# Projection products between the transposes of attention, and products of 512 columns in halves

## The chip, the cores and the metric

The kernel runs on one core of one Trainium2 chip. Its engines are named as in the profile: PE is TensorE (matmuls), PEld its weight loads, DVE is VectorE, ACT is ScalarE, POOL is GpSimd, and SP only issues transfers. The metric is the device time of one execution in microseconds, as the median of the runs; lower is better. Before the change it was 425.61 us, the median of three runs from 425.08 to 425.87.

## The reference: what is computed

One decoder block on x of 512 rows by 1024 columns, all in float32:

```python
h = rms_norm(x, norm_g)
proj = h @ w_in          # fq fk fv fz mq mk mv mz (512 each), ga gb (1024 each), fl (8)
y_fox  = fox_attention(rms(fq), rms(fk), fv, log_sigmoid(fl + b_f)) * silu(fz)
y_moba = moba_attention(rope(rms(mq)), rope(rms(mk)), mv) * silu(mz)
merged = sigmoid(ga + b_gate[0]) * (y_fox @ w_fox) + sigmoid(gb + b_gate[1]) * (y_moba @ w_moba)
out = x + merged @ w_out
```

Each branch has 8 heads of width 64. Both attentions are causal over 512 positions. With 512 positions and three blocks chosen out of two, the block choice of the second branch leaves plain causal attention.

## The kernel before, in words

**Number format.** TensorE multiplies in a reduced float32 format. So each operand is split into a high part and a low part, and every product of two matrices is three matmuls into the same accumulator: high by high, high by low, low by high. In the text "product" is one such matmul. A product of 256 columns has a moving side of 128 x 256, one of 512 columns a moving side of 128 x 512; the stationary side is always 128 x 128 and is loaded by a weight load of its own (PEld).

**Units.** The projections are cut into units. A unit of q, k or v (`unit`) takes 128 rows of the input and 256 weight columns: 8 chunks of the contraction by 3 products are 24 products of 256 columns, into one accumulator bank of the pair `pj`, and then a copy out by ACT and DVE. A unit of the z columns (`unit_z`) takes 128 weight columns and all 512 rows: 24 products of 512 columns. A unit of the w_fox product (`unit_f`) is 12 products of 512 columns. Before a unit, `pump` issues the loads and splits of the weight chunks that are due up to three chunks ahead of it.

**Attention.** It goes in four groups: heads 0 to 3 of the first branch ("fa"), heads 4 to 7 ("fb"), then the same of the second branch ("ma", "mb"). A group consists of pieces. `Tr` turns q and k of two heads by 8 transposes of 128 x 128 into two banks (`p_qT`, `p_kT`, L530 and L532), from which ACT and DVE make QS, KH and KL (L539 to L547). `Aa` computes the logits of a head in four row blocks (`lg`, L572 and L573), the softmax numerators with DVE (L575) and Exp on ACT (L577). `Bb` turns the numerators by 10 transposes of 128 x 128 (`p_a` four, `p_b` four, `p_cc` two, L617), splits them (`pth` by ACT at L623, `ptl` by DVE at L624) and multiplies them with v (`pv`, L627 and L628). `Yp` normalises and multiplies with the z gate. A transpose is a matmul whose stationary side is the data and whose moving side is an identity of 128 columns.

**What sets the order.** The program mixes the pieces of a group with the units listed for it: `inter` alternates between the two lists in proportion to their lengths, a whole unit or a whole piece at a time. Group fa is filled with units of fqb, fkb, fvb and mqa; fb with mka, mva and mza; ma with mqb, mkb and mvb; mb with mzb (two units of 512 columns) and wf0 to wf2 (six). The units of wf3 follow alone. The program's order is then the order of preference only: when the kernel is built, a scheduler puts the instructions of each engine in the order in which it expects their inputs, so that in the built program products of a unit already stand between logits and pv matmuls. `behind(engine)`, that is `tc.issue_after`, ties an instruction to stand after the last one given to that engine so far. Every engine, TensorE too, works off its instructions in the built order, and waits at an instruction whose inputs are not ready.

**After attention** come the gate products (`pb_GA`, `pb_GB`, L767 to L770), the w_moba product (`pm`) and the output product (`po`).

Of the kernel before, what the change touches and what calls it, by code (L numbers as in the profile page):

```python
# [13 lines left out]
P = 128  # L14
# [15 lines left out]
def fox_moba_kernel(ctx: ExitStack, tc, xT, x, w_in, w_fl, w_fox, w_moba, w_out, cst, rope, out):  # L30
# [60 lines left out]
    def col(c, n=1):  # L91
        return cs[:, c:c + n]
# [212 lines left out]
        for i, (a, b) in enumerate(pairs):  # L305
            T.matmul(o, a, b, start=(i == 0), stop=(i == n - 1))

    def unit_mm(p, name, t, hfs=(0, 1), first=True, last=True):
        n = 264 if name == "fka" else CW
        for hf in hfs:  # L310
            hi, lo = chunks[name][hf]
            for k in range(4):
                kk = 4 * hf + k
                st = slice(t * P, (t + 1) * P)
                T.matmul(p[:, :n], Gh[:, kk, st], hi[:, k, :n], start=(kk == 0), stop=False)
                T.matmul(p[:, :n], Gh[:, kk, st], lo[:, k, :n], start=False, stop=False)
                T.matmul(p[:, :n], Gl[:, kk, st], hi[:, k, :n], start=False, stop=(kk == KT - 1))

    def evac_qk(p, name, t):
        if name not in QN:  # L320
# [75 lines left out]
    def unit(name, t):  # L396
        def go():
            p = pj(f"pj_{name}{t}")
            unit_mm(p, name, t)
            if name[1] == "v":  # L400
                evac_v(p, name, t)
            else:
                evac_qk(p, name, t)
        return go


    def tr_mm(p, name, c):
        cc = slice(c * P, (c + 1) * P)
        for hf in range(2):
            hi, lo = chunks[name][hf]  # L410
            for k in range(4):
                kk = 4 * hf + k
                gh, gl = Z[kk] if name[0] == "f" else (Gh[:, kk, :], Gl[:, kk, :])
                T.matmul(p, hi[:, k, cc], gh, start=(kk == 0), stop=False)
                T.matmul(p, hi[:, k, cc], gl, start=False, stop=False)
                T.matmul(p, lo[:, k, cc], gh, start=False, stop=(kk == KT - 1))

    ZS = {}

# [2 lines left out]
    def unit_z(name, c):  # L422
        def go():
            p = (tp if name == "fzb" else pj)(f"pz_{name}{c}")
            tr_mm(p, name, c)
            z = t2("y", 15, f"zs_{name}{c}")
            s = t2("y", 15, "sg") if name == "mzb" else t2("u", 4, "sg")
            if name[0] == "f":
                V.tensor_tensor(out=z, in0=p, in1=rbc, op=OP.mult)
                A.activation(s, z, AF.Tanh, scale=0.5)  # L430
                V.scalar_tensor_tensor(z, s, 1.0, z, op0=OP.add, op1=OP.mult)
            else:
                A.activation(s, p, AF.Tanh, scale=0.5)
                V.scalar_tensor_tensor(z, s, 1.0, p, op0=OP.add, op1=OP.mult)
            ZS[name[0], 2 * (name[2] == "b") + c] = z
        return go


    LR = con.tile([64, S], F32R, name="LR")
# [77 lines left out]
    def attn_group(br, half, gq, gk):  # L517
# [8 lines left out]
        def Tr(pr):  # L526
            def go():
                pq, pk = tp("p_qT"), tp("p_kT")
                for t in range(NT):
                    T.transpose(pq[:, t * P:(t + 1) * P], qn[:, t, pr * P:(pr + 1) * P], ident)  # L530
                for t in range(NT):
                    T.transpose(pk[:, t * P:(t + 1) * P], kn[:, t, pr * P:(pr + 1) * P], ident)  # L532
                for o in range(2):
                    h = 2 * pr + o
                    me, ot = (slice(0, HD), slice(HD, P)) if o == 0 else (slice(HD, P), slice(0, HD))
                    qs = t2("qs", 4, "QS", dt=F32R)
                    kh = t2("qs", 4, "KH", dt=F32R)
                    kl = KLt[o][pr]
                    A.activation(qs[me, :], pq[me, :], AF.Copy, scale=gq[me, :])  # L539
                    V.scalar_tensor_tensor(qs[ot, :], pq[me, :], gq[me, :], qs[me, :].bitcast(F32),  # L540
                                           op0=OP.mult, op1=OP.subtract)
                    A.activation(kh[me, :], pk[me, :], AF.Copy, scale=gk[me, :])
                    if direct:
                        A.activation(kh[ot, :], pk[me, :], AF.Copy, scale=gk[me, :])  # L544
                    else:
                        nc.scalar.dma_start(out=kh[ot, :].bitcast(F32), in_=kh[me, :].bitcast(F32))
                    V.scalar_tensor_tensor(kl[me, :], pk[me, :], gk[me, :], kh[me, :].bitcast(F32),  # L547
                                           op0=OP.mult, op1=OP.subtract)
                    q2 = qs
                    if fox:  # L550
                        q2 = Q2t[o]
                        lr = slice(HD, HD + 4) if o == 0 else slice(0, 4)
                        hh = hb + h
                        nc.sync.dma_start(out=q2[lr, :].bitcast(F32), in_=LR[hh:32:8, :].bitcast(F32))
                        nc.sync.dma_start(out=kl[lr, :].bitcast(F32), in_=LR[32 + hh:64:8, :].bitcast(F32))
                        if direct:
                            V.tensor_copy(q2[me, :], qs[me, :].bitcast(F32))
                        else:
                            nc.scalar.dma_start(out=q2[me, :].bitcast(F32), in_=qs[me, :].bitcast(F32))
                    st[h] = (qs, kh, kl, q2)  # L560
            return go
# [48 lines left out]
        def Bb(h):  # L610
            def go():
# [2 lines left out]
                pv = pst("pv", 1, "pv")  # L614

                def blk(dst, i, j):
                    T.transpose(dst, pts[i][:, j * P:(j + 1) * P], ident)  # L617

                def spl(p, n):
                    tag, w, bufs = ("pt", 512, 4) if n == 512 else ("pc", 256, 2)  # L620
# [67 lines left out]

    FS, MG = {}, {}

    def br_mm(p, name, br, c):
        hi, lo = chunks[name][0]
        cc = slice(c * P, (c + 1) * P)
        for k in range(4):
            yh, yl = Y[br, k]
            T.matmul(p, hi[:, k, cc], yh, start=(k == 0), stop=False)  # L696
            T.matmul(p, hi[:, k, cc], yl, start=False, stop=False)  # L697
            T.matmul(p, lo[:, k, cc], yh, start=False, stop=(k == 3))  # L698

    def unit_f(i, c):  # L700
        def go():
            j = 2 * i + c
            p = pj(f"pf{j}")
            br_mm(p, f"wf{i}", "f", c)
            if j == 0:
                f = sb.tile([P, 4, S], F32, name="f03", tag="v", bufs=2)
                FS[0], FS[1] = f[:, 0:2, :], f[:, 2:4, :]
            elif j in (4, 6):
                FS[j // 2] = sb.tile([P, 2, S], F32, name=f"f{j}", tag="qk", bufs=4)
            A.activation(FS[i][:, c, :], p, AF.Copy)  # L710
        return go
# [121 lines left out]
    def merge_a(i, c):  # L833
        if True:
            j = 2 * i + c
            p = pj(f"pm{j}")
            br_mm(p, f"wm{i}", "m", c)
            u = SG[i][:, c, :]
            V.tensor_tensor(out=u, in0=p, in1=u, op=OP.mult)
            V.tensor_tensor(out=u, in0=u, in1=FS[i][:, c, :], op=OP.add)  # L840
# [180 lines left out]
            return [unit_z(name, c) for c in range(2)]  # L1021
        return [unit(name, t) for t in range(4)]

    def filler(names):
        res = []
        for nm in names:
            for n, u in enumerate(units(nm)):
                def go(i=first_prep[nm] + (n if nm[0] == "G" else 0), u=u):
                    pump(i)
                    u()  # L1030
                res.append(go)
        return res

    def inter(a, b):
# [30 lines left out]
    for k, u in enumerate(fz):  # L1065
        u()
        if k < 3:
# [7 lines left out]
            ("f", "b", C_FQ, C_FK, ["mka", "mva", "mza"]),  # L1075
            ("m", "a", C_MQ, C_MK, ["mqb", "mkb", "mvb"]),
            ("m", "b", C_MQ, C_MK, ["mzb", "wf0", "wf1", "wf2"]))
    head, body, tail, gate = attn_group("f", "a", col(C_FQ), col(C_FK))
    head[0]()
    for n in range(4):  # L1080
        nxt = []

        def following(n=n, nxt=nxt):
            br, half, cq, ck = plan[n + 1][:4]
            if n == 1:
                moba_begin()
            nxt.extend(attn_group(br, half, col(cq), col(ck)))
            nxt[0][0]()
        fill = filler(plan[n][4])
        if n == 0:  # L1090
            for k in range(4):
                store = []

                at = 3 * k

                def with_sums(u=fill[at], k=k, store=store):
                    u()
                    with tc.issue_after(last_on(mybir.EngineType.DVE)):
                        store.append(make_sums(k))

                def with_store(u=fill[at + 1], store=store):
                    u()
                    store[0]()
                fill[at], fill[at + 1] = with_sums, with_store
        inter(body + ([following] if n < 3 else []) + tail, fill)
        if n < 3:
            at = 2
            body, tail = nxt[1][:at] + gate + nxt[1][at:], nxt[2]
            gate = nxt[3]
    seq(["wf3"])  # L1110
    enter("gates")
    load_sums()
    fill = filler(["GA0", "GA1", "GB0"])
# [123 lines left out]
```

## Time and profile before

| What | Value |
|---|---|
| median of three runs | 425.61 us |
| the profiled execution, in all | 425.94 us |
| its span, first to last instruction | 424.2 us |
| granted TensorE clock | 0.999 |
| busy PE, PEld, DVE, ACT, POOL | 417.8, 388.6, 327.4, 279.2, 103.8 us |
| matmuls recorded | 2913 |
| attention stage, about | 66 to 285 us |

The page lists busy time by engine, then the span in 40 slices, the transfers, the chain of work that ended last, and groups of instructions. A group's row gives the line, engine and operation, what is written from what, the shapes and the count, then busy time and the mean of one in ns, then the engine's idle time before them and what ended it. A row of the timeline begins with the start in us from the span's start and the duration in us; several equal instructions in a row are one row with a count. Matmuls overlap in the records and their ends are modelled, so what a matmul takes is read from the distance between starts. A row of busy time by stretch gives the stretch and its length, then busy time and count for each engine, the granted clock, the share of the transfer engines and GB/s.

### The profile page before, as it was taken

What the parts mean: (1) busy time and instruction counts of PE and PEld (TensorE: products, weight loads), DVE (VectorE), ACT (ScalarE), POOL (GpSimd) and SP (SyncE); (2) the same over time, 40 slices, a digit from 0 to 9 for tenths busy, and PEclk for the clock granted to TensorE, in tenths of its full rate; (3) what the DMA queues carried; (4) which work ended last, traced back from release to release, by engine and by line L of the source; (5) the groups of instructions that cost most, each with busy time, mean ns of one, the idle gap of its engine ahead of it and who ended that gap; (6) DMA issues with size and microseconds to landing.
All of it is one profiled execution on the core that took longest, in us unless ns stands there. A gap on an engine that the chain in (4) does not pass through costs nothing.

```text
span 424.2 us, 7682 instructions
## 1 busy us (share of the span) xinstructions
PE 417.8 (98%) x2913; PEld 388.6 (92%) x2913; DVE 327.4 (77%) x574; ACT 279.2 (66%) x527; POOL 103.8 (24%) x120
## 2 busy tenths in 40 slices
PE   8999999999999999999999999999999999999996
PEld 6998899999999998899998888899999989988885
DVE  3779977799967778678666679767979698689883
ACT  4976326778777878569757687656756535686450
POOL 1065630225235550015660100340000000022230
PEclk9999999999999999999999999999999999999999
DMA  7972334667253033212032310673052703697484
GB/s 233 392 281 87 112 100 111 181 206 199 74 176 114 26 102 100 80 45 99 27 100 68 106 53 27 229 250 117 24 178 62 236 2 110 208 259 118 99 140 159
DMA packets 24340, 56.10 MB, mean 132 GB/s; under 512 B 2808, under 2 KB 7600, under 8 KB 24304
## 3 DMA queue, kind: packets, MB, share of 16 engines
q1 hardware_dynamic: 13392, 38.11, 27.9%
q0 software_dynamic: 3392, 8.39, 8.7%
q10 hardware_dynamic: 7520, 9.11, 6.7%
q8 instruction: 23, 0.38, 0.4%
q14 instruction: 13, 0.11, 0.1%
HBM read 48.11 MB, written 6.32 MB: 128 GB/s over the span
## 4 chain that ended last, share of the span: by engine, by line
PE 96%; DMA 1%; SPq 0%; DVE 0%; issue 0%; ACT 0%
PE pb_GB L770 3%; PE pb_GA L770 3%; PE pb_GA L767 3%; PE pb_GB L767 3%; PE pb_GB L769 3%; PE pb_GA L769 3%; PE po L958 3%; PE po L957 3%; PE po L956 3%; PE pv L628 2%; PE lg L573 2%; PE pv L627 2%; PE lg L572 2%; PE pf L697 2%; PE pf L696 2%; PE pm L698 2%
## 5 line engine op out<-in xcount | busy, mean ns | idle before, releaser
L343 POOL TENSOR_TENSOR ff<-ss,mh 128x8 f32<-128x8 f32 x16 | 31.6, 1981 | 71.4 <-DVE ss L341 62.9
L575 DVE CUSTOM_DVE_ANT_0 p<-lg,mask 128x128 f32<-128x128 f32 (+1 forms) x64 | 30.9, 487 | 16.1 <-PE lg L573 15.6
L577 ACT ACTIVATE p<-p,negm 128x128 f32<-128x128 f32 (+1 forms) x64 | 35.7, 559 | 10.9 <-DVE negm L575 10.0
L905 POOL DMA_DIRECT2D wr_o<-in_w_out_dram x4 | 4.9, 1294 | 95.5 <-ACT wr_o L904 95.5
L143 DVE TENSOR_TENSOR wl_GA<-wr_ga,wh_GA 128x1024 fp32r<-128x1024 f32 x14 | 16.9, 1223 | 5.8 <-ACT wh_GA L141 3.9
L141 ACT ACTIVATE wh_GA<-wr_ga 128x1024 fp32r<-128x1024 f32 x14 | 14.7, 1061 | 9.9 <-PE pb_GA L769 5.1
L141 ACT ACTIVATE wh_GB<-wr_gb 128x1024 fp32r<-128x1024 f32 x14 | 14.6, 1059 | 9.5 <-PE pm L697 3.5
L918 ACT ACTIVATE wh_o<-wr_o 128x1024 fp32r<-128x1024 f32 x14 | 14.8, 1060 | 7.9 <-PE pb_GB L769 2.8
L572 PE MATMUL lg<-KH,QS 128*128 128x128 f32 (+1 forms) x64 | 20.0, 324 | 0.0
L919 DVE TENSOR_TENSOR wl_o<-wr_o,wh_o 128x1024 fp32r<-128x1024 f32 x14 | 17.0, 1222 | 3.8 <-ACT wh_o L918 3.8
L143 DVE TENSOR_TENSOR wl_GB<-wr_gb,wh_GB 128x1024 fp32r<-128x1024 f32 x14 | 16.9, 1222 | 3.5 <-ACT wh_GB L141 3.5
L653 DVE TENSOR_TENSOR ypair<-pv,ysh 64x512 f32<-64x512 f32 x16 | 11.0, 687 | 6.7 <-ACT ysh L652 6.3
L547 DVE SCALAR_TENSOR_TENSOR KL<-p_kT,cs,KH 64x512 fp32r<-64x512 f32 x16 | 12.0, 749 | 3.4 <-ACT KH L544 3.2
L652 ACT ACTIVATE ysh<-pv 64x512 f32<-64x512 f32 x16 | 9.5, 594 | 7.3 <-PE pv L628 4.2
L624 DVE TENSOR_TENSOR ptl<-p_a,pth 128x512 fp32r<-128x512 f32 x16 | 11.0, 685 | 4.2 <-ACT pth L623 4.2
L337 DVE TENSOR_REDUCE ss<-sq 128x8 f32<-128x512 f32 x16 | 10.9, 681 | 4.0 <-ACT sq L336 3.9
L767 PE MATMUL pb_GA<-Gh,wh_GA 128*128 128x256 f32 x48 | 13.6, 284 | 0.0
L769 PE MATMUL pb_GA<-Gl,wh_GA 128*128 128x256 f32 x48 | 13.5, 281 | 0.0
L770 PE MATMUL pb_GA<-Gh,wl_GA 128*128 128x256 f32 x48 | 13.5, 281 | 0.0
L770 PE MATMUL pb_GB<-Gh,wl_GB 128*128 128x256 f32 x48 | 13.5, 281 | 0.0
L769 PE MATMUL pb_GB<-Gl,wh_GB 128*128 128x256 f32 x48 | 13.4, 281 | 0.0
L767 PE MATMUL pb_GB<-Gh,wh_GB 128*128 128x256 f32 x48 | 13.3, 281 | 0.0
(461 smaller groups left out, 1801.8 us busy)
## 6 DMA issues: line engine op xcount, KB each, us to landing
wr_ga<-in_w_in_dram SPq DMA_DIRECT2D x8, 512.0 KB, 3.8
wr_gb<-in_w_in_dram SPq DMA_DIRECT2D x8, 512.0 KB, 4.6
wr_o<-in_w_out_dram SPq DMA_DIRECT2D x8, 512.0 KB, 11.4
xt<-in_xT_dram SPq DMA_DIRECT2D x8, 256.0 KB, 7.3
x<-in_x_dram SPq DMA_DIRECT2D x8, 256.0 KB, 6.0
s_dramh<-sum_sh ACTq DMA_DIRECT2D x8, 256.0 KB, 5.6
s_draml<-sum_sl ACTq DMA_DIRECT2D x8, 256.0 KB, 2.5
wr_wf<-in_w_fox_dram SPq DMA_DIRECT2D x4, 512.0 KB, 3.2
```

Of the source, the lines that this page charges most:

```text
L141: A.activation(hi[:, :, 0:n], src, AF.Copy)
L143: eng.tensor_tensor(out=lo[:, q, 0:n], in0=src[:, q], in1=hi[:, q, 0:n].bitcast(F32), op=OP.subtract)
L343: G.tensor_tensor(out=f2, in0=ss.rearrange("p t h -> p (t h)"), in1=mh, op=OP.pow)
L572: T.matmul(lg[:, :n], qs[:, qt], kh[:, :n], start=True, stop=False)
L575: V.tensor_tensor_reduce(pt, lg[:, :n], mask[:, 512 - n:512], -0.125, 3.0e38, op0=OP.add, op1=OP.min, accum_out=mkn[:, hh, i:i + 1])
L577: A.activation(pt, pt, AF.Exp, bias=mkn[:, hh, i:i + 1], scale=-1.0, accum_out=rs[:, hh, i:i + 1])
L767: T.matmul(o, hi[:, k, cc], lh, start=(n < 3 and c == 0 and k == 0), stop=False, skip_group_check=True)
L769: T.matmul(o, hi[:, k, cc], ll, start=False, stop=False, skip_group_check=True)
L770: T.matmul(o, lo[:, k, cc], lh, start=False, stop=(k == 3), skip_group_check=True)
L918: A.activation(wide(hi), wide(R[key, c]), AF.Copy)
L919: V.tensor_tensor(out=wide(lo), in0=wide(R[key, c]), in1=wide(hi).bitcast(F32), op=OP.subtract)
L956: T.matmul(o, gh, hi[:, c, r, :], start=(new and k == 0), stop=False, skip_group_check=True)
```

## The change

1. The functions that issue products of units become generators: they hand over one product at a time. `products` issues them as before; `halves` issues each product of 512 columns as two of 256 columns, on the two halves of the same bank and with the same stationary side. `halves` is used for mzb and for all of wf0 to wf3; mza and the z units before attention stay whole, as do the products of w_moba.
2. The units of all four groups are made before attention and also put into one list, `AHEAD`, in their order. `turn` replaces the calls of transpose in `Tr` and `Bb`. After each transpose it gives out up to three products of the first unfinished unit in that list; with the last of them come the unit's copies. All transposes but the first of a `Tr` or a `Bb` are tied to stand behind the last TensorE instruction so far, which as a rule is the third such product. The products themselves are not tied: the scheduler may put them elsewhere. A unit begun in this way is finished when its turn comes in `inter`; one that is already done then issues nothing, except that `pump` is called for it at that place.

```diff
-    def unit_mm(p, name, t, hfs=(0, 1), first=True, last=True):
+    def unit_mm(name, t):
         n = 264 if name == "fka" else CW
...
+        st = slice(t * P, (t + 1) * P)
+        for kk in range(KT):
+            hi, lo = (w[:, kk % 4, :n] for w in chunks[name][kk // 4])
+            gh, gl = Gh[:, kk, st], Gl[:, kk, st]
+            yield from ((gh, hi), (gh, lo), (gl, hi))
+
+    def halves(p, pairs):
+
+        pairs = list(pairs)
+        n = 2 * len(pairs)
+        for i in range(n):
+            a, b = pairs[i // 2]
+            c = slice(i % 2 * CW, (i % 2 + 1) * CW)
+            if i:
+                yield
+            T.matmul(p[:, c], a, b[:, c], start=(i == 0), stop=(i >= n - 2), skip_group_check=True)
+
+    def products(o, pairs):
+
+        pairs = list(pairs)
+        for i, (a, b) in enumerate(pairs):
+            if i:
+                yield
+            T.matmul(o, a, b, start=(i == 0), stop=(i == len(pairs) - 1))
...
     def unit(name, t):
         def go():
             p = pj(f"pj_{name}{t}")
-            unit_mm(p, name, t)
+            yield from products(p[:, :264 if name == "fka" else CW], unit_mm(name, t))
...
     def unit_z(name, c):
         def go():
             p = (tp if name == "fzb" else pj)(f"pz_{name}{c}")
-            tr_mm(p, name, c)
+            yield from (halves if name == "mzb" else products)(p, tr_mm(name, c))
...
+    AHEAD = []
+
+    def turn(o, i, first):
+        if first:
+            T.transpose(o, i, ident)
+        else:
+            with behind(mybir.EngineType.PE):
+                T.transpose(o, i, ident)
+        for n in range(3):
+            while AHEAD and AHEAD[0].done:
+                AHEAD.pop(0)
+            if AHEAD:
+                AHEAD[0].step()
+
+    class Unit:
+        def __init__(self, i, go):
+            self.i, self.go, self.it, self.done = i, go, None, False
+
+        def step(self):
+            if self.it is None:
+                self.it = self.go()
+            if self.it is None or next(self.it, self) is self:
+                self.done = True
+
+        def run(self):
+            pump(self.i)
+            while not self.done:
+                self.step()
...
                 for t in range(NT):
-                    T.transpose(pq[:, t * P:(t + 1) * P], qn[:, t, pr * P:(pr + 1) * P], ident)
+                    turn(pq[:, t * P:(t + 1) * P], qn[:, t, pr * P:(pr + 1) * P], t == 0)
                 for t in range(NT):
-                    T.transpose(pk[:, t * P:(t + 1) * P], kn[:, t, pr * P:(pr + 1) * P], ident)
+                    turn(pk[:, t * P:(t + 1) * P], kn[:, t, pr * P:(pr + 1) * P], False)
...
                 def blk(dst, i, j):
-                    T.transpose(dst, pts[i][:, j * P:(j + 1) * P], ident)
+                    turn(dst, pts[i][:, j * P:(j + 1) * P], j == 0 and i == 0)
...
     def unit_f(i, c):
         def go():
             j = 2 * i + c
             p = pj(f"pf{j}")
-            br_mm(p, f"wf{i}", "f", c)
+            yield from halves(p, br_mm(f"wf{i}", "f", c))
...
-    def filler(names):
+    def filler(names, ahead=False):
         res = []
         for nm in names:
             for n, u in enumerate(units(nm)):
-                def go(i=first_prep[nm] + (n if nm[0] == "G" else 0), u=u):
-                    pump(i)
-                    u()
-                res.append(go)
+                x = Unit(first_prep[nm] + (n if nm[0] == "G" else 0), u)
+                if ahead:
+                    AHEAD.append(x)
+                res.append(x.run)
         return res
...
+    fills = [filler(p[4], True) for p in plan]
+    wf3 = filler(["wf3"])
...
-        fill = filler(plan[n][4])
+        fill = fills[n]
...
-    seq(["wf3"])
+    for u in wf3:
+        u()
```

More of the change, by code (lines that the diff above doesn't have):

```diff
@@ L306, in mm3 @@
             T.matmul(o, a, b, start=(i == 0), stop=(i == n - 1))
-    def unit_mm(p, name, t, hfs=(0, 1), first=True, last=True):
+    def unit_mm(name, t):
         n = 264 if name == "fka" else CW
[L310 to L317, printed above, removed]
+        st = slice(t * P, (t + 1) * P)
[18 more added lines that the diff above has]
+            T.matmul(o, a, b, start=(i == 0), stop=(i == len(pairs) - 1))
     def evac_qk(p, name, t):
@@ L404, in unit, with tr_mm @@
         return go
-    def tr_mm(p, name, c):
+    def tr_mm(name, c):
         cc = slice(c * P, (c + 1) * P)
[L409 to L416, printed above, removed]
+        for kk in range(KT):
+            hi, lo = (w[:, kk % 4, cc] for w in chunks[name][kk // 4])
+            gh, gl = Z[kk] if name[0] == "f" else (Gh[:, kk, :], Gl[:, kk, :])
+            yield from ((hi, gh), (hi, gl), (lo, gh))
     ZS = {}
@@ L689, in fox_moba_kernel, with br_mm @@
     FS, MG = {}, {}
-    def br_mm(p, name, br, c):
+    def br_mm(name, br, c):
         hi, lo = chunks[name][0]
@@ L695, in br_mm @@
             yh, yl = Y[br, k]
-            T.matmul(p, hi[:, k, cc], yh, start=(k == 0), stop=False)
-            T.matmul(p, hi[:, k, cc], yl, start=False, stop=False)
-            T.matmul(p, lo[:, k, cc], yh, start=False, stop=(k == 3))
+            yield from ((hi[:, k, cc], yh), (hi[:, k, cc], yl), (lo[:, k, cc], yh))
     def unit_f(i, c):
@@ L836, in merge_a @@
             p = pj(f"pm{j}")
-            br_mm(p, f"wm{i}", "m", c)
+            for _ in products(p, br_mm(f"wm{i}", "m", c)):
+                pass
             u = SG[i][:, c, :]
```

## The prediction

> **What bounds the kernel now.** I read the profile in this order: the page's busy table and chain, then who waited for whom on TensorE, then the busy time by stretch, then single rows of the timeline, to price each kind of step.
>
> ```profile
> span 424.2 us, 7682 instructions
> PE 417.8 (98%) x2913; PEld 388.6 (92%) x2913; DVE 327.4 (77%) x574; ACT 279.2 (66%) x527; POOL 103.8 (24%) x120
> PEclk9999999999999999999999999999999999999999
> PE 96%; DMA 1%; SPq 0%; DVE 0%; issue 0%; ACT 0%
> ```
>
> TensorE is busy for 98% of the span and carries 96% of the chain that ended last, at a full granted clock. The list of what TensorE waited for has three rows only, all at lines of the head of the kernel:
>
> ```profile
> PE warm_ps L107 <- DVE fg_pre L480: 1.5, 1, 1.5
> PE fqa L392 <- DVE wl_fqa L168: 0.7, 1, 0.7
> PE fqa L391 <- ACT Zh L131: 0.6, 1, 0.6
> ```
>
> The attention stage, where the change lies, has this busy time in its four head groups (columns: us, then PE, PEld, DVE, ACT, POOL busy):
>
> ```profile
> 66.00:118.00 52.00, 52.00 (x427) 51.22 (x426) 46.91 (x101) 40.66 (x88) 13.00 (x9) 1.00 0.56 161
> 118.00:172.00 54.00, 54.00 (x408) 51.53 (x408) 40.59 (x87) 42.14 (x90) 22.19 (x30) 1.00 0.30 98
> 172.00:225.00 53.00, 53.00 (x419) 51.37 (x418) 35.41 (x77) 37.69 (x83) 21.48 (x26) 1.00 0.22 70
> 225.00:285.00 60.00, 60.00 (x349) 52.25 (x349) 45.31 (x85) 44.04 (x91) 10.31 (x12) 1.00 0.37 123
> ```
>
> TensorE never waits there: 219 of 219 us. So there is no stall for a new order to close, and the time changes only by what a step costs on TensorE, or by a stall that the new order opens. DVE in the first group (46.91 of 52) is the nearest cover to give way.
>
> **What one step costs.** Ends of matmuls are modelled, so I use differences of starts. Products, first and last of runs of one width:
>
> ```profile
> 53.78 0.28 PE L315 MATMUL pj_fva<-wh_fva,Gh 128*128 128x256 f32 x1
> 59.92 0.28 PE L316 MATMUL pj_fva<-wl_fva,Gh 128*128 128x256 f32 x1
> ...
> 236.68 0.40 PE L414 MATMUL pz_mzb<-Gh,wh_mzb 128*128 128x512 f32 x1
> 240.18 0.40 PE L414 MATMUL pz_mzb<-Gh,wh_mzb 128*128 128x512 f32 x1
> ...
> 290.74 0.28 PE L769 MATMUL pb_GA<-Gl,wh_GA 128*128 128x256 f32 x1
> 333.22 0.28 PE L770 MATMUL pb_GB<-Gh,wl_GB 128*128 128x256 f32 x1
> ```
>
> 52 steps of 256 columns in 6.14 us are 0.1181 us each; 358 in the gates stage in 42.48 us are 0.1187; 15 steps of 512 in the last head group in 3.50 us are 0.2333. Transposes, ten and four in a row between products of 256, then one alone between products of 512 (with a stationary side of 8 columns), and last the step of 384 columns:
>
> ```profile
> 96.72 0.28 PE L317 MATMUL pj_fkb<-wh_fkb,Gl 128*128 128x256 f32 x1
> 96.84 0.60 PE L617 MATMUL p_a<-ident,p 128*128 128x128 f32 x4
> 97.27 0.60 PE L617 MATMUL p_b<-ident,p 128*128 128x128 f32 x4
> 97.71 0.38 PE L617 MATMUL p_cc<-ident,p 128*128 128x128 f32 x2
> 97.85 0.37 PE L315 MATMUL pj_fvb<-wh_fvb,Gh 128*128 128x256 f32 x1
> 98.05 0.28 PE L316 MATMUL pj_fvb<-wl_fvb,Gh 128*128 128x256 f32 x1
> ...
> 123.62 0.29 PE L317 MATMUL pj_mqa<-wh_mqa,Gl 128*128 128x256 f32 x1
> 123.74 0.60 PE L617 MATMUL p_a<-ident,p 128*128 128x128 f32 x4
> 124.30 0.28 PE L315 MATMUL pj_mqa<-wh_mqa,Gh 128*128 128x256 f32 x1
> ...
> 174.77 0.39 PE L628 MATMUL pv<-ptl,v_fvb 128*128 128x512 f32 x1
> 175.00 0.27 PE L597 MATMUL p_ri<-ident,rinv 128*8 128x128 f32 x1
> 175.34 0.39 PE L414 MATMUL pz_mza<-Gh,wh_mza 128*128 128x512 f32 x1
> ...
> 235.08 0.34 PE L572 MATMUL lg<-KH,QS 128*128 128x384 f32 x1
> 235.25 0.34 PE L573 MATMUL lg<-KL,QS 128*128 128x384 f32 x1
> ```
>
> From 96.72 to 98.05 are 1.33 us; less two products of 256 (0.236) that is 1.094 for ten, 0.109 each. From 123.62 to 124.30 it is 0.68 less 0.236, 0.444 for four, 0.111 each. From 174.77 to 175.34 it is 0.57 less two products of 512 (0.467): 0.10 for one alone. So a transpose costs about 0.11 us wherever it stands, though its 128 columns would stream in 0.06: steps of 256, 384 and 512 take 0.118, 0.17 and 0.233, some 0.058 more for each 128. The reason is in the rows of weight loads:
>
> ```profile
> 123.64 0.46 PEld L617 LDWEIGHTS p_a<-ident,p 128*128 128x128 f32 x4
> ...
> 174.54 0.19 PEld L628 LDWEIGHTS pv<-ptl,v_fvb 128*128 128x128 f32 x1
> 174.77 0.08 PEld L597 LDWEIGHTS p_ri<-ident,rinv 128*8 128x8 f32 x1
> 175.00 0.19 PEld L416 LDWEIGHTS pz_mza<-Gh,wl_mza 128*128 128x128 f32 x1
> ```
>
> The load for 174.77 is over after 0.08 us, and the next load starts only at 175.00, when the transpose itself starts. Loads run one ahead and no further, so the load behind a transpose cannot hide under the long product before it.
>
> **The change part by part.** (a) *Halves.* In the built order the matmuls of 512 columns fall from 602 to 458 and those of 256 rise from 1840 to 2128: 144 products (48 of mzb, 96 of wf0 to wf3) become 288. Both halves have the same stationary side; the page counts 2913 loads for 2913 matmuls although the products at L414 and L415 follow each other on the same wh, so I count a load for every half. A pair costs 2 x 0.1187 against 0.2333, +0.0041 us; times 144 that is +0.59 us. I take the gates row, since there too the stationary side is a weight and the moving side the input. By the projection row it is 2 x 0.1181 - 0.2333 = 0.0029, +0.42; the end below is 0 (the columns are the same), the one above 0.0064 x 144 = +0.92, should the 512s it replaces run at the 0.2314 that they show elsewhere:
>
> ```profile
> 31.56 0.39 PE L414 MATMUL pz_fza<-Zh,wh_fza 128*128 128x512 f32 x1
> 53.55 0.39 PE L416 MATMUL pz_fzb<-Zh,wl_fzb 128*128 128x512 f32 x1
> ```
>
> (95 steps in 21.99 us.)
>
> (b) *Products behind transposes.* Both orders hold 243 transposes; before they stand in 62 unbroken runs (most of 4, five of 10), after in 150, of which 115 are of one. Total work is the same; only the edges of runs multiply, by 88. The edge has a price: the load of the four at 123.64 starts 0.02 after the product at 123.62, where the loads at 174.77 and 175.00 start with the matmul before them; the first transpose stands at 123.74, 0.12 after the product. Ten in a row at 1.094 and four at 0.444 give 0.108 per transpose and 0.011 per run, with rounding as large as the edge. I take 0.006 per run, about half: 88 x 0.006 = +0.53 us; ends 0 and 0.011 x 88 = +0.97. A transpose behind a product of 384 or 512 shows no edge (0.10 above), but only about 20 of the 150 runs stand so.
>
> (c) *Moved work.* The first projection products start earlier, and the transposes of a head spread over up to nine gaps of three products (9 x 0.354 = 3.2 us). What reads them, the copies at L623 and L624 and QS and KH at L539 to L547, starts that much later, and the pv and lg matmuls behind those. TensorE works in one order, so a transpose that waits for its Exp (L577) now holds the products tied in behind it, and a pv that waits holds the next unit. I cost this at nothing: projection products still stand between, and the waits list shows TensorE never reaching a transpose, pv or lg too soon. The price without that cover is the second rival. ACT, DVE, POOL and SP keep their operations; SP and POOL get no new transfer, and a weight chunk is read at most a few products earlier than before.
>
> Sum: 0.59 + 0.53 = +1.12 us. The profiled execution took 425.94 us in all (span 424.2), so 427.06 for one like it; the median of the three runs is 425.61, 0.33 below, so 426.7. A difference of 0.2%, 0.85 us, is about what a measurement of this kernel tells from no change.
>
> The Trainium skill, page "TensorE: Matmul & The Clock Gate", section "Back-to-back issue gap", says that loads and matmuls are pipelined through a 64-deep reorder window and that a stream at 128 columns runs at about 81 ns a matmul. By that figure 150 transposes whose following load is hidden would cost 0.029 us less each, an estimate of -4.3 us, against +0.53 by the rows. The trace does not agree: 0.109 each in the run of ten, and the load at 175.00 waited.
>
> **The rivals.** *Hidden loads (faster).* If two loads could be ahead, three products and a transpose would cost four loads, 4 x 0.109 = 0.436, and not 3 x 0.118 + 0.111 = 0.465: -0.029 for 127 such places, -3.7, with the halves -3.1: 422.5 us. It decides as soon as the load behind a transpose starts before that transpose. Against it stands the row at 175.00; for it, only that the one such row quoted has an 8-column load.
>
> *A stall in the first group (slower).* DVE is busy for 90% of it, and each head passes three copies at L624:
>
> ```profile
> L624 DVE TENSOR_TENSOR ptl<-p_a,pth 128x512 fp32r<-128x512 f32 x16 | 11.0, 685 | 4.2 <-ACT pth L623 4.2
> ```
>
> If the spread transposes make half such a copy late (0.34 us) for each of four heads, TensorE waits 1.4 us at pv: 428.1. In the other groups DVE and ACT have more than 11 us to spare.
>
> *Hardly anything happens (within 0.2%).* The products are only offered; the build decides, and 93 of 181 pairs of neighbouring transposes remain. If an edge costs nothing and the halves 0.42, the time is 426.0.
>
> **How the numbers follow.** No stall, steps as priced: 0.60, 426.7 with its own range 426.1 to 427.5. A stall besides: 0.15, 428.1. Edges free: 0.14, 426.0. Hidden loads: 0.11, 422.5. The range 425.3 to 428.6 leaves out the last case and little else. About a sixth of the first case lies under +0.85 us; with the third that gives 0.24 for no visible change, 0.65 for slower, 0.11 for faster.
>
> **What would show it.** Right: the list of TensorE's waits still ends with the head of the kernel, a single transpose between products of 256 costs 0.11 to 0.12, two halves 0.236 to 0.238, the end of the gates run (333.22 before) comes about 1.1 us later, and the rest of the span is as long as before. Wrong: a weight load that starts before the transpose ahead of it (faster), a row for pv, lg or pf in TensorE's waits (slower still), or halves that share a load, 144 loads fewer than matmuls.

## The result, and the profile after

The changed kernel took 428.26 us (median of 4 runs, 428.07 to 428.45), the kernel before 425.58 us (median of 4 runs on the same chip, 425.08 to 425.87). The ratio is 1.0064, with a 95% interval of 1.0047 to 1.0082: 2.68 us slower, where 1.12 was forecast.

First the page of the changed kernel: its busy times and the chain that ended last (the span is 426.5 us).

```profile
PE 419.7 (98%) x3057; PEld 396.0 (93%) x3057; DVE 328.4 (77%) x574; ACT 278.7 (65%) x527; POOL 106.4 (25%) x120
PE 91%; DVE 3%; DMA 3%; ACT 1%; issue 1%; SPq 0%; ACTq 0%; DVEq 0%
```

TensorE still is the bound. There are 3057 loads for 3057 matmuls, so no half shares a load. But the chain, which was 96% TensorE with 1% in transfers, now runs for 3% through DVE and for 3% through transfers. The list of what TensorE waited for (us in total, times, longest) names the places:

```profile
PE warm_ps L107 <- DVE fg_pre L523: 1.5, 1, 1.5
PE fqa L408 <- DVE wl_fqa L168: 0.6, 1, 0.6
PE lg L615 <- DMA KH<-KH: 0.5, 1, 0.5
PE pv L671 <- DVE ptl L667: 0.4, 1, 0.4
PE fqa L407 <- ACT Zh L131: 0.2, 1, 0.2
```

The third and fourth rows are new; the others are those of the head. By stretch (PE, PEld, DVE, ACT, POOL busy):

```profile
66.00:118.00 52.00, 51.13 (x415) 49.92 (x415) 43.47 (x95) 38.00 (x84) 12.40 (x9) 1.00 0.54 161
...
172.00:225.00 53.00, 53.00 (x415) 51.25 (x413) 38.19 (x81) 38.32 (x86) 22.58 (x26) 1.00 0.23 70
```

Both waits lie in the first group. TensorE is idle for 0.87 us of it, and DVE does 3.4 us less in these 52 us than before (46.91), so some of its work slips into the groups behind (the third has 38.19, before 35.41).

The first product of pj_fva starts anywhere from 52.98 to 53.90 us in the traces of this case. To compare traces without this luck of the head, I take the length from that product to the last matmul. Before it begins at 53.78 (quoted in the prediction) and ends with

```profile
420.30 0.28 PE L958 MATMUL po<-wh_o,mg 128*128 128x256 f32 x1
```

which is 366.52 us; after, from

```profile
53.33 0.28 PE L333 MATMUL pj_fva<-wh_fva,Gh 128*128 128x256 f32 x1
...
422.62 0.28 PE L1000 MATMUL po<-wh_o,mg 128*128 128x256 f32 x1
```

it is 369.29: +2.77 us, against +2.68 by the medians. The steps themselves, in the timeline of the changed kernel: single transposes with three products behind each, and pairs of halves (x2). Here and below "..." stands for rows left out.

```profile
66.06 0.27 PE L459 MATMUL p_qT<-ident,qn_fqa 128*128 128x128 f32 x1
66.06 0.19 PEld L333 LDWEIGHTS pj_fqb<-wh_fqb,Gh 128*128 128x128 f32 x1
...
67.92 0.27 PE L459 MATMUL p_kT<-ident,qn_fka 128*128 128x128 f32 x1
...
243.40 0.40 PE L325 MATMUL pz_mzb<-Gh,wl_mzb 128*128 128x256 f32 x2
...
244.82 0.40 PE L325 MATMUL pz_mzb<-Gh,wl_mzb 128*128 128x256 f32 x2
```

Four places of one transpose and three products take 1.86 us, 0.465 each; less 0.354 for the products this is 0.111 for the transpose. The load behind the transpose starts with it (both 66.06), not ahead of it. Six pairs of halves take 1.42 us, 0.237 each.

**The wait at lg.** Before, the four transposes of p_kT stand in a row; KH is copied from them, and a transfer copies KH to the other 64 partitions:

```profile
66.47 0.60 PE L532 MATMUL p_kT<-ident,qn_fka 128*128 128x128 f32 x4
...
68.03 0.68 ACT L542 ACTIVATE KH<-p_kT,cs 64x512 fp32r<-64x512 f32 x1
...
68.79 0.86 ACTq L546 DMA_DIRECT2D KH<-KH  x1
...
74.80 0.28 PE L315 MATMUL pj_fqb<-wh_fqb,Gh 128*128 128x256 f32 x1
...
74.92 0.22 PE L572 MATMUL lg<-KH,QS 128*128 128x128 f32 x1
...
75.09 0.33 PE L572 MATMUL lg<-KH,QS 128*128 128x256 f32 x1
```

After, the last of the four ends 2.1 us later (69.13, before 67.07), KH starts 1.14 and the issue of the transfer 1.09 later. Counted from the first product of pj_fva, which starts 0.45 us earlier here, the issue is 1.54 later (16.55 us behind it, before 15.01). And lg waits:

```profile
68.86 0.27 PE L459 MATMUL p_kT<-ident,qn_fka 128*128 128x128 f32 x1
...
69.17 0.68 ACT L585 ACTIVATE KH<-p_kT,cs 64x512 fp32r<-64x512 f32 x1 [1.18 <-PE p_kT L459]
...
69.88 0.48 ACTq L589 DMA_DIRECT2D KH<-KH  x1
...
75.00 0.28 PE L333 MATMUL pj_fqb<-wh_fqb,Gl 128*128 128x256 f32 x1
...
75.76 0.30 PE L615 MATMUL lg<-KH,QS 128*128 128x128 f32 x1 [0.47 <-DMA KH<-KH]
...
76.18 0.33 PE L615 MATMUL lg<-KH,QS 128*128 128x256 f32 x1
```

From the last product to the third lg (the one of 256 columns at L615) it is 1.18 us, where before it was 0.29: 0.89 lost. In the chain of the changed kernel (start, length, what) the transfer is one long piece:

```profile
69.88 5.74 DMA KH<-KH
```

It lands at 75.62. The trace of the kernel before has the last completion signal of the same transfer at 74.52, 5.72 us after its issue and 0.40 ahead of the lg at 74.92. So the landing came 1.10 later; 0.40 of that was slack, and TensorE itself reached lg 0.20 later (75.12, one step behind the product at 75.00), which leaves a wait of 0.50. Another 0.14 passed until lg started and 0.25 until the third lg: 0.89 together.

**The wait at pv.** Before, the second half of p_b is ready well ahead of its reader: DVE writes ptl from 104.40 to 105.08, pv reads it at 106.08.

```profile
101.59 0.61 ACT L623 ACTIVATE pth<-p_b 128x512 fp32r<-128x512 f32 x1
...
104.40 0.68 DVE L624 TENSOR_TENSOR ptl<-p_b,pth 128x512 fp32r<-128x512 f32 x1
...
106.08 0.42 PE L628 MATMUL pv<-ptl,v_fva 128*128 128x384 f32 x1
```

After, the copy at L666 starts at 103.10, 1.51 later, and is done at 103.70. But ptl starts only at 105.95, 1.55 later than before, because DVE first finishes two operations at L143 and one each at L278 and L353. In the rows of the timeline:

```profile
102.18 2.65 DVE L143 TENSOR_TENSOR wl_mqa<-wr_mqa,wh_mqa 128x1024 fp32r<-128x1024 f32 x2
...
103.10 0.60 ACT L666 ACTIVATE pth<-p_b 128x512 fp32r<-128x512 f32 x1
...
104.75 0.68 DVE L278 TENSOR_TENSOR sum_sl<-sum_sf,sum_sh 128x512 fp32r<-128x512 f32 x1
...
105.36 0.67 DVE L353 TENSOR_REDUCE ss<-sq 128x8 f32<-128x512 f32 x1
...
105.84 0.27 PE L456 MATMUL p_qT<-ident,qn_fqb 128*128 128x128 f32 x1
105.87 0.42 PE L670 MATMUL pv<-pth,v_fva 128*128 128x384 f32 x1
105.95 0.67 DVE L667 TENSOR_TENSOR ptl<-p_b,pth 128x512 fp32r<-128x512 f32 x1
...
106.55 0.41 DVE L369 TENSOR_TENSOR v_fvb<-pj_fvb,v_fvb 128x256 fp32r<-128x256 f32 x1
...
106.68 0.44 PE L671 MATMUL pv<-ptl,v_fva 128*128 128x384 f32 x1 [0.39 <-DVE ptl L667]
...
106.96 0.22 PE L670 MATMUL pv<-pth,v_fva 128*128 128x128 f32 x1
```

From the transpose at 105.84 to the row at 106.96 it is 1.12 us, where a transpose (0.11) and two steps of 384 columns (0.34) take 0.45: 0.67 lost. Before, six transposes of p_qT and p_kT stood near this pv; now they are tied to products of pj_fvb, whose buffer DVE frees only with the copy at 106.55.

The chain shows that this is more than one late copy. Between 88.1 and 106.6 us it does not touch TensorE at all: it runs over DVE (11.1 us), ACT (4.6) and the gaps between their instructions, and ends at this pv.

```profile
88.14 0.04 DVE p L618
...
106.03 0.61 DVE ptl L667
...
106.68 0.44 PE pv L671
```

So here DVE, which the prediction named as the cover nearest to giving way, is together with ACT the path for 18.5 us.

### The profile page after: what moved, and what is told of

Its sections match the earlier page's. It is cut to its first block, busy times and chain, and to the rows that moved or that the text cites. A ratio compares the mean times of both kernels' runs of the same rounds, so it can differ in the third digit from the quotient of the medians.

```text
span 426.5 us, 7965 instructions
## 1 busy us (share of the span) xinstructions
PE 419.7 (98%) x3057; PEld 396.0 (93%) x3057; DVE 328.4 (77%) x574; ACT 278.7 (65%) x527; POOL 106.4 (25%) x120
## 4 chain that ended last, share of the span: by engine, by line
PE 91%; DVE 3%; DMA 3%; ACT 1%; issue 1%; SPq 0%; ACTq 0%; DVEq 0%
PE pf L325 5%; PE pm L333 5%; PE pb_GB L811 3%; PE pb_GA L811 3%; PE pb_GB L808 3%; PE pb_GA L808 3%; PE pb_GB L810 3%; PE pb_GA L810 3%; PE po L1000 3%; PE po L999 3%; PE po L998 3%; PE pj_fva L333 3%; PE pj_mqb L333 3%; PE pj_mka L333 3%; PE pz_mzb L325 3%; PE pj_mqa L333 3%
## 5 line engine op out<-in xcount | busy, mean ns | idle before, releaser
L141 ACT ACTIVATE wh_GB<-wr_gb 128x1024 fp32r<-128x1024 f32 x14 | 14.6, 1058 | 9.5 <-PE pm L333 3.5
L143 DVE TENSOR_TENSOR wl_GA<-wr_ga,wh_GA 128x1024 fp32r<-128x1024 f32 x14 | 17.1, 1240 | 4.7 <-ACT wh_GA L141 3.4
L615 PE MATMUL lg<-KH,QS 128*128 128x128 f32 (+1 forms) x64 | 19.8, 325 | 0.5 <-DMA KH<-KH 0.5
L141 ACT ACTIVATE wh_GA<-wr_ga 128x1024 fp32r<-128x1024 f32 x14 | 14.6, 1059 | 7.7 <-PE pb_GA L810 6.0
L143 DVE TENSOR_TENSOR wl_GB<-wr_gb,wh_GB 128x1024 fp32r<-128x1024 f32 x14 | 16.8, 1221 | 3.5 <-ACT wh_GB L141 3.5
L585 ACT ACTIVATE KH<-p_kT,cs 64x512 fp32r<-64x512 f32 x16 | 10.9, 682 | 6.7 <-PE p_kT L459 6.5
L583 DVE SCALAR_TENSOR_TENSOR QS<-p_qT,cs,QS 64x512 fp32r<-64x512 f32 x16 | 12.0, 750 | 3.3 <-ACT QS L582 2.9
L353 DVE TENSOR_REDUCE ss<-sq 128x8 f32<-128x512 f32 x16 | 10.8, 678 | 4.0 <-ACT sq L352 3.9
L325 PE MATMUL pf<-yhf,wh_wf 128*128 128x256 f32 x64 | 13.8, 292 | 0.0
L325 PE MATMUL pf<-ylf,wh_wf 128*128 128x256 f32 x64 | 13.8, 291 | 0.0
```

Source lines behind the costliest of these rows:

```text
L141: A.activation(hi[:, :, 0:n], src, AF.Copy)
L143: eng.tensor_tensor(out=lo[:, q, 0:n], in0=src[:, q], in1=hi[:, q, 0:n].bitcast(F32), op=OP.subtract)
L325: T.matmul(p[:, c], a, b[:, c], start=(i == 0), stop=(i >= n - 2), skip_group_check=True)
L615: T.matmul(lg[:, :n], qs[:, qt], kh[:, :n], start=True, stop=False)
```

## The experiments

Differences are to the kernel before, timed on the same chip; "length" is the stretch from the first product of pj_fva to the last matmul, against 366.52.

| kernel | median us (kernel before) | ratio, 95% interval | difference us | length us |
|---|---|---|---|---|
| changed kernel | 428.26 (425.58) | 1.0064, 1.0047 to 1.0082 | +2.68 | +2.77 |
| halves_only | 425.82 (425.18) | 1.0013, 1.0004 to 1.0022 | +0.64 | +0.57 |
| ahead_whole | 431.19 (425.18) | 1.0129, 1.0110 to 1.0148 | +6.01 | +5.91 |
| fa_plain | 426.48 (425.18) | 1.0030, 1.0019 to 1.0041 | +1.30 | +1.11 |
| untied | 426.68 (425.18) | 1.0029, 1.0018 to 1.0040 | +1.50 | +1.35 |
| head_plain | 427.02 (425.43) | 1.0040, 1.0028 to 1.0053 | +1.59 | +1.62 |
| direct_after | 427.01 (425.43) | 1.0036, 1.0023 to 1.0049 | +1.58 | +1.72 |
| last_one_whole | 427.42 (425.43) | 1.0047, 1.0034 to 1.0059 | +1.99 | +1.93 |
| one_product_whole | 426.21 (425.43) | 1.0015, 1.0006 to 1.0024 | +0.78 | +0.61 |

Each length is from one trace, and the two columns of differences lie up to 0.19 us apart. So the terms of 0.2 to 0.4 us below, and the price of an edge, are remainders of that quality.

**halves_only**: the halves without products behind transposes.

```
     def turn(o, i, first):
-        if first: ... else: (tied)
-        for n in range(3): ... AHEAD[0].step()
+        T.transpose(o, i, ident)
```

> Only the halves: mzb and wf0 to wf3 as 288 products of 256 columns, transposes as before in 62 runs, nothing given out behind them. My theory (of the 2.68 us by which the changed kernel is slower, 0.6 are halves, 0.4 edges of runs, 1.6 to 1.8 are three waits of TensorE): +0.6 us against before, 426.2, and no wait on TensorE after the head. Rival (the halves themselves bring waits, since a bank is written twice as often): +1.5 us or more, with a row for pf or pz in TensorE's waits.

The length grew by 0.57 us, 0.0040 for each of the 144 products cut in two, and TensorE's waits were the three of the head alone. Term (a) stands (0.59).

**ahead_whole**: the products behind transposes, without halves.

```
-            yield from (halves if name == "mzb" else products)(p, tr_mm(name, c))
+            yield from products(p, tr_mm(name, c))
...
-            yield from halves(p, br_mm(f"wf{i}", "f", c))
+            yield from products(p, br_mm(f"wf{i}", "f", c))
```

> Only the products behind transposes; mzb and wf stay whole products of 512 columns. My theory, if the built order of the last group stays good: +2.1 us against before (edges 0.4, waits 1.7), 427.7. Rival: the last group has only 120 products to give out in place of 240, they run out before its last heads, and TensorE waits at pv there: +3.5 us or more, with a long wait near 280 us; then the halves are what the last group needs to be covered, not a cost alone.

It is 6 us slower, not 2.1: the rival came, with more than its 3.5 us. To the two waits of the first group comes a third, in the last; the row of that wait, and the rows around it:

```profile
PE pv L670 <- DVE ypair L696: 2.4, 1, 2.4
```

```profile
281.58 0.38 PE L459 MATMUL p_cc<-ident,p 128*128 128x128 f32 x2
...
284.32 0.79 PE L670 MATMUL pv<-pth,v_mvb 128*128 128x512 f32 x1 [2.37 <-DVE ypair L696]
```

Three whole products behind each transpose are twice the columns of three halves: the products of the last group are given out before its last head, and nothing is left between the last p_cc and a pv that waits for DVE. The 2.4 us of the wait are not the whole price. In the stretch that follows (columns as above) the granted clock is 0.52, where it is 1.00 from 278 to 284:

```profile
284.00:287.00 3.00, 2.68 (x9) 2.49 (x10) 0.60 (x2) 0.00 (x0) 1.56 (x3) 0.52 1.01 367
```

The eight pv steps from 284.32 to 286.83 take 2.51 us; the same eight of the head before, from 279.42 on, take 1.37. So the halves, which cost 0.57 us as steps, are also cover.

**last_one_whole**: whole products, three behind each transpose in the first three groups, one in the last.

```
+    EACH = [3]
...
-        for n in range(3):
+        for n in range(EACH[0]):
...
+        EACH[0] = 1 if n == 3 else 3
```

(with the two edits of ahead_whole)

> No halves, three products behind each transpose in the first three groups, one in the last. Theory (with whole products the last group had run out of products to put ahead of its last pv): no pv wait of more than 0.3 us from 240 us on, and the time is that of the changed kernel less the halves: 1.9 to 2.3 us over the kernel before, with the lg and pv waits of the first group as they are. Rival (the last group waits because any spreading makes its last heads late): a pv wait of 1 us or more near 280 us stays, and the time is 3 us or more over the kernel before.

No wait is left from 240 us on and the time is +1.99. The two waits of the first group are there too, the one at lg longer and the one at pv shorter than in the changed kernel:

```profile
PE lg L616 <- DMA KH<-KH: 0.8, 1, 0.8
...
PE pv L672 <- DVE ptl L668: 0.2, 1, 0.2
```

So the wait behind 281.58, and the slow steps after it, came of running out of products, and the last group needs no halves when one product goes behind each transpose.

**fa_plain**: the transposes of the first group in rows and untied, and with them the first `Tr` of the second, which is issued within the first; the others as changed.

```
+    PLAIN = [True]
...
-        if first:
+        if first or PLAIN[0]:
...
-        for n in range(3):
+        for n in range(0 if PLAIN[0] else 3):
...
+        PLAIN[0] = n == 0
```

> As the changed kernel, but in the first head group transposes stand as before, untied and with nothing behind them. My theory: both waits of the first group (lg at L615 for the transfer of KH, pv at L671 for ptl, together 1.55 us) go, and about 33 edges (0.13): +1.0 us against before, 426.6. Rival (the waits are an accident of the profiled run, or move on to the next group): +2.3 us or more.

Both waits are gone, and with them (and with 33 of the 88 new edges) 1.66 us of the length. What is left, +1.11, is 0.57 for the halves, 0.29 at one place near 246 us where a product behind a single transpose starts late and the trace names no releaser (the changed kernel has the same near 248: 0.32 us from the transpose to the product, where other places have 0.03), and 0.25 for 55 more runs of transposes: 0.005 each.

**untied**: the transposes not tied to the products behind them.

```
-        if first:
-            T.transpose(o, i, ident)
-        else:
-            with behind(mybir.EngineType.PE):
-                T.transpose(o, i, ident)
+        T.transpose(o, i, ident)
```

> As the changed kernel, but no transpose is tied to the instruction before it. If giving out the products is what delays QS, KH and ptl: the waits stay, +2.3 to +2.7 us against before. If the ties are what delays them (a tied transpose cannot pass a product that the build would have put later): both waits go, and +1.0 us remains.

The pv wait is gone and lg waits for about half as long:

```profile
PE lg L611 <- DMA KH<-KH: 0.2, 1, 0.2
```

The time, +1.50, lies between the two that were expected. Each theory held in part: without the ties the build puts other work where TensorE would wait (six transposes stand ahead of this lg), but KH still comes late.

**head_plain**: only the eight transposes of the first head pair in a row.

```
-        for n in range(3):
+        for n in range(0 if PLAIN[0] else 3):
...
+        PLAIN[0] = False
```

(with PLAIN as in fa_plain; it becomes False once these eight are issued)

> Only the eight transposes of the first head pair of the first group stand in a row, as before; all the others have three products offered behind them and are tied. Theory (two waits add to the steps: one at the first lg, because those eight transposes are spread and KH goes through a transfer, and one at a pv, because the transposes of p are spread): the wait of about 0.8 us at lg near 75 us goes, the wait of about 0.7 us at pv near 106 us stays, and the time is 1.8 to 2.1 us over the kernel before. Rival (the first group is late as a whole, whichever transposes are spread): lg still waits, at a later head, and the time stays 2.5 to 2.9 us over the kernel before.

The lg wait is gone, as the theory had it. The pv wait, which should have stayed, is gone too, and so the time, +1.59, is below the 1.8 expected; in place of the pv wait a product waits for its buffer, at the same point of the group:

```profile
105.54 0.41 DVE L369 TENSOR_TENSOR v_fvb<-pj_fvb,v_fvb 128x256 fp32r<-128x256 f32 x1
105.66 0.27 PE L457 MATMUL p_qT<-ident,qn_fqb 128*128 128x128 f32 x1
...
106.09 0.36 PE L333 MATMUL pj_fvb<-wh_fvb,Gh 128*128 128x256 f32 x1 [0.16 <-DVE v_fvb L369]
106.29 0.28 PE L333 MATMUL pj_fvb<-wl_fvb,Gh 128*128 128x256 f32 x1
```

It is 0.63 from the transpose to the second product instead of 0.23 (0.111 for a transpose and 0.118 for a step), 0.40 lost. The late work is DVE's in either case; whether it shows at pv or at the tied product depends on the order.

**direct_after**: in the first group too, ACT and DVE write the second copies of KH and QS, in place of transfers.

```
-        direct = br + half != "fa"
+        direct = True
```

> The changed kernel, with the second copies of KH and QS of the first group written by ACT and DVE in place of two transfers, as in the other groups. Theory (lg waits for the transfer of KH, which takes longer than a copy): lg no longer waits near 75 us, and the time falls by about 0.8 us, to 1.7 to 2.1 us over the kernel before; a pv wait of 0.4 to 1.0 us stays. Rival (KH is late because the transposes ahead of it are, and DVE is full in the first group): lg or pv still waits, now for ACT or DVE, with 1.5 us or more in all, and the time is 2.7 us or more over the kernel before.

The lg wait is gone although all transposes are spread, and the first lg stands at 71.93, 3.8 us earlier than in the changed kernel: the transfers held it. The run replaces those of KH and QS at once; that it was the one of KH, the trace of the changed kernel says. The pv wait that was expected to stay is gone here as well, and the time is a little below the 1.7 expected. What is left is again the tied product that waits for DVE:

```profile
PE pj_fvb L333 <- DVE v_fvb L369: 0.3, 1, 0.3
```

**one_product_whole**: no halves, one product behind each transpose.

```
-        for n in range(3):
+        for n in range(1):
```

(with the two edits of ahead_whole)

> No halves, one product behind each transpose everywhere: 145 runs of transposes, 109 of one, nearly as many as with three products. Theory (the edges of the runs cost 0.004 us each, and the waits come from the length of the spread): no lg or pv wait of over 0.3 us, and 83 x 0.004 = 0.3 us over the kernel before, at most 0.6. Rival (the ties and the edges themselves make the waits): lg or pv waits of 1 us or more in all stay, and the time is 1.5 us or more over the kernel before.

With 145 runs of transposes, 109 of them of one, and all ties in place, TensorE waits in the head alone. The length grew by 0.61; 0.19 of it is one late product near 152 us, and 0.42 for 83 edges is 0.005 each. By the medians it is +0.78, above the 0.6 that was expected at most.

The first head shows why one product is harmless. Before, ACT was busy with L141 and L539 when the last p_kT ended (67.07), and took it up 0.96 us later, at 68.03. With one product behind each transpose this p_kT comes 0.85 us later, counted from the first product of pj_fva (53.46 here), and that fits: the transfer is issued 15.01 us behind that product, as before.

```profile
68.47 0.86 ACTq L589 DMA_DIRECT2D KH<-KH  x1
```

With three products the last p_kT comes 2.51 us later by the same count, and the transfer 1.54. So neither the ties nor the edges make the long waits by themselves; how far the transposes are spread does.

No version was faster than the kernel before: every part of the change adds steps or waits to an engine that had no gap to fill.

## Why the prediction was right and where it failed

The direction was right, and the time, 428.26, lies in the range of 425.3 to 428.6, near its upper end. The point value was 1.6 us too low, and the main case's own range, 426.1 to 427.5, was missed: the wide range held because it took in the stall at 428.1, not because the sum was right. Term by term, of the 2.77 us by which the length grew:

| term | forecast us | measured us |
|---|---|---|
| (a) 144 products in halves | +0.59 | +0.57 |
| (b) 88 more edges of runs of transposes | +0.53 | +0.35 (what is left) |
| (c) moved work: lg behind the transfer of KH | 0 | +0.89 |
| (c) moved work: pv behind ptl | 0 | +0.67 |
| (c) one late product near 248 us | 0 | +0.29 |

*What bounds the kernel* was right: with no gap on TensorE before, nothing could be gained. *(a)* was right, with a load for every half. (Its upper end is mis-added: 2 x 0.1187 - 0.2314 is 0.0060 and not 0.0064, so +0.86 and not +0.92; nothing hangs on it.) The Trainium skill, page "TensorE: Matmul & The Clock Gate", section "Wait — 56ns, not 53.3ns?", gives a warm matmul a time in proportion to its columns and a fixed 2.5 ns or so besides, so that a cut in two costs one such fixed part, by the page an estimate of 144 x 2.5 ns = 0.36 us. The trace agrees in kind, with 0.0040 us a cut. *(b)* was right in kind: a single transpose costs 0.111 and an edge, by what is left over, 0.004 to 0.005 in three kernels, where I took 0.006.

*The step that failed* is (c): "I cost this at nothing: projection products still stand between, and the waits list shows TensorE never reaching a transpose, pv or lg too soon." A list without waits shows no slack. Read from the rows, the slack was small at both places. The first head's transfer of KH landed 0.40 us ahead of its lg, while the spread of eight transposes delayed its landing by 1.10. At pv ptl was done 1.0 us early, and it came 1.55 later, at the end of a chain of 18.5 us over DVE and ACT. I had counted the delay, up to 3.2 us, and held it against no slack at all. What was put at nothing measured 0.89 + 0.67 + 0.29 = 1.85 us. I also wrote that SP and POOL get no new transfer, and overlooked that an old one, issued by ACT, starts later with the copy that feeds it.

*The rivals.* The stall in the first group, given 0.15 at 428.1, is what happened, in its place and with its engine for one of two waits. Its size was right by chance: one pv that loses 0.67 and not four that lose 0.34, and an lg that waits for a transfer, which it did not name. *Hidden loads* fell: the load behind a transpose starts with it, 3057 loads for 3057 matmuls, and no run was faster. With that the estimate that the prediction drew from the Trainium skill, page "TensorE: Matmul & The Clock Gate", section "Back-to-back issue gap", by which the spread should have gained, is not borne out by any run here. *Hardly anything happens* fell with the edges and the waits. Of the signs named beforehand, the row for pv and lg in TensorE's waits was the one that came.

What stays open: in head_plain, direct_after and untied the pv wait went although the transposes of p were still spread, together with a change of order. So the runs show that it hangs on the length of the spread, the ties and the order. The chain names the operations ahead of ptl (the second at L143, then L278 and L353), but no run moved one of them alone. The late product near 248 us has no cause in the trace.

## What to carry to other kernels

Where an engine shows no waits, a new order can only add steps or open waits; before costing moved work at nothing, read the slack of its first readers row by row, from the last producer to the reader, and hold the delay against it, transfers included. Products offered ahead of time are cover taken from later: count how many are left at the last place that needs them. Offer the least that fills the gap: one product behind each transpose opened no long wait where three opened two; in the first head its delay fitted into the time for which ACT was busy anyway.

## What the runs showed that was not expected

The transfer that copies KH from one half of the partitions to the other, 128 KB, holds the chain for 5.74 us from its issue, and in the nine traces that have it the first one takes 5.56 to 6.30 us to its last completion signal; in direct_after ACT writes the same data in 0.69 us:

```profile
69.60 0.69 ACT L587 ACTIVATE KH<-p_kT,cs 64x512 fp32r<-64x512 f32 x1
```

And cutting products in halves, which costs 0.57 us as steps, saved more than 3 us where products ran short: ahead_whole is +6.01 where the changed kernel is +2.68. Part of that is the lower clock (0.52 granted from 284 to 287 us) behind a wait of 2.4 us.
